# RWKV-7 in a hybrid backbone: the two directions of a chunk, instead of two chunks, on the two partition halves

## The chip, the cores and the metric

One core of a Trainium2 chip runs the whole network in one launch. The metric is the device time of one execution in microseconds (us). The engines are named as in the profile: PE (TensorE), ACT (ScalarE), DVE (VectorE), POOL (GpSimd) and SP (SyncE, which issues nearly all DMAs here).

## The reference, cut to what matters

Two layers of a hybrid block work on 512 latent and 256 context tokens of width 2048. One input projection feeds four branches (S5, windowed attention, RWKV-7, Hyena), each 512 wide, and an output projection merges them. The change touches RWKV alone. It has 8 heads of 64 channels and runs over time in both directions; per step and head, with state `S` (64 x 64):

```python
sa = jnp.einsum('bhij,bhj->bhi', state, -kk_t)
state = (state * w_t[:, :, None, :] + sa[..., None] * b_t[:, :, None, :]
         + v_t[..., None] * k_t[:, :, None, :])
y = jnp.einsum('bhij,bhj->bhi', state, r_t)
```

The context is run first, from a zero state, then the latents from the state that it leaves. The backward direction does the same over reversed time, and the two outputs are added.

## The kernel before

All matrices are f32. Where the trace counts matmul records, an f32 product of RWKV has two records and the split products of the projections (high and low parts, line 1645) have one each.

**RWKV in blocks.** The recurrence is computed in chunks of 64 steps. A block is two heads (128 channels, one of 4 channel tiles `c`) times 256 tokens (one of 3 groups `g`: context, first and second half of the latents), for both directions: 12 blocks per layer, 24 in all. Each block has three stages, `features`, `invert` and `chain`, and `run` traces them block after block. Most tiles have two buffers, so the stages of the next block may run ahead.

**`features`** (lines 288 to 368) loads r, k, kk, v (`ld`) and the half logits (`la`), makes decays with scans along time (line 312), scaled keys `kb` (lines 331, 332), then the scores `S`: per block 16 products of 64 contracted rows, 128 weight columns and 128 moving columns (line 340). For each direction `d` and head `h` four products lie on one half of the array's rows (`tile_position=(h * 64, 0)`), into one of two PSUM banks `mA`; DVE masks each bank into `S` (line 342). Then twelve 128 x 128 transposes (lines 351 to 353) go to `KU` by DVE and ACT (355 to 358), and 16 small products (line 365) give `BV`, through ACT (line 367). In these last the two parities `b` of chunk alternate between two quarters of the array, with rows and columns of 64 each, and all write one bank.

**`invert`** (lines 377 to 424) inverts the triangular scores: 31 steps of two operations on POOL (lines 398, 399) between DMAs that regroup the data, and 32 small products.

**`chain`** (lines 426 to 483) goes over the four chunks of a block in order, with the state `cur`. Before the change a pair of chunks (parities `b` 0 and 1) shares the 128 partitions, the even one's rows on one half, the odd one's on the other, and both directions of a chunk lie on the same half. Per chunk: two products of the state, one per direction, both into the same 64 output columns (line 439, here called fp); a DVE addition into `BV` (line 441); four products with the inverse, all on one quarter of the array (line 446, here called up); an ACT copy with the sign turned into `KU` (line 448); four products that make the state's increment (line 459, sp), whose two heads alternate between column halves; two DVE additions into the new state (line 466, with the decay at line 454); and the outputs y (lines 472, 475). fp, up and sp use one bank, `mU`, in turn.

**Order.** A planner that simulates the program fixes the order of each engine's instructions before the run. The class `Pace` adds order by hand: while RWKV runs, the input projections of the next branches (line 1645, three matmuls to a unit) fill PE, and a unit may not stand ahead of a given number of RWKV steps: fp, up and sp of each chunk count as steps (`lead`), the first step of a block allows 33 units in layer 0 and 27 in layer 1, every other 3 and 1. The weights of the filling units are split into high and low parts by ACT (line 1484) and by DVE or POOL (line 1485).

Of the kernel before, what the change touches and what calls it, by code (L numbers as in the profile page):

```python
# [37 lines left out]
# columns of the packed RWKV parameters  # L38
# [15 lines left out]
def pack_rw(I):  # L54
# [5 lines left out]
    wa = np.stack([I["rw_w2"], I["rw_a2"]], axis=2)  # layer, direction, (w, a), row, output  # L60
# [3 lines left out]
class K:  # L64
# [51 lines left out]
    def ring(self, shape=(128, 512)):  # L116
        """The banks beside those of the input projection, in turn."""
# [3 lines left out]
    def rms(self, y, sq, tmp, eng, eps, gate=None):  # L121
        """1 / sqrt(mean square + eps) over 4 channel tiles y, in sq (all of one width). With gate, which runs beside it: half of that, from 4 eps."""
# [19 lines left out]
class Pace:  # L142
    """Issue order on the tensor engine: units of a filling stream issue behind steps of a leading one."""
# [4 lines left out]
    def step(self, ins, allow):  # L148
        """ins leads; the units that come before it grow by allow."""
# [20 lines left out]
class RwFeed:  # L170
    """Token shift of the RWKV projections; r, k, kk, v and the half logits kept in both orders of time."""

    def __init__(self, k, l, raw):
# [5 lines left out]
        # 1 - mu_prev - mu_next, w0 / 2, a0 / 2, k_a / 2, 1 - k_a, 2 - k_a  # L179
# [11 lines left out]
        # r, k, kk, v and tanh of the half logits (decay, a), forward and reversed  # L191
# [7 lines left out]
    def store(self, d, z, ctx):  # L199
        """z [128, 769] (latent | - | context) into d [128, 2, NT], as it is and reversed."""  # L200
# [8 lines left out]
    def feed(self, j, lat, ctx):  # L209
        """Projection tile j (r 0-3, k 4-7, v 8-11, lora 12) in lat / ctx [128, n]: token shift."""  # L210
# [30 lines left out]
    def logits(self, lz):  # L241
        """tanh of half the decay and a logits of all channels: (high, low, high, low) x (high, high, low, low) in one product. In 8 parts."""
# [30 lines left out]
class Rwkv:  # L273
    """Bidirectional RWKV-7 over chunks of 64 steps; both directions advance together, each in its own order of time."""
# [13 lines left out]
    def features(self, c, g):  # L288
        """Scores and transposed operands of 4 chunks of two heads."""
# [10 lines left out]
        BV = t([128, 2, 4, 64], "rwBV", self.nbuf)  # L300
# [25 lines left out]
        # slots of a pair: K even | B even | B odd | K odd, in the place of k and kk  # L326
        kb = ld[:, 1:3].rearrange("p q d t -> p (q d t)").rearrange("p (x s t) -> p x s t", x=4, s=4)
        r4 = "p d (a b s) -> p (d a) b s"
        pi4 = pi.rearrange(r4, a=2, b=2)
        a4, kd4 = a.rearrange(r4, a=2, b=2), kd.rearrange(r4, a=2, b=2)  # L330
        V.tensor_tensor(kb[:, :, 1:3, :], a4, pi4, ALU.mult)
        V.tensor_tensor(kb[:, :, 0::3, :], kd4, pi4, ALU.mult)
# [10 lines left out]
        pc = PC.rearrange("p d (a b) -> p (d a) b", b=2).unsqueeze(3).to_broadcast([128, 4, 2, 64])  # L343
        # end-scaled K (natural), B (chunks of a pair exchanged)
        V.tensor_tensor(kd4, kb[:, :, 0::3, :], pc, ALU.mult)
        V.tensor_tensor(a4[:, :, ::-1, :], kb[:, :, 1:3, :], pc, ALU.mult)
        for d in range(2):
            for p in range(2):
                x = slice(p * 128, p * 128 + 128)
                pt = k.bank("mA", 2)  # L350
                nc.tensor.transpose(pt[:, 0:128], kd[:, d, x], C["ident"])
                nc.tensor.transpose(pt[:, 128:256], v[:, d, x], C["ident"])
                nc.tensor.transpose(pt[:, 256:384], a[:, d, x], C["ident"])
                ku = KU[:, d, p]
                V.tensor_copy(ku[0:64, 0], pt[0:64, 0:256].rearrange("p (a b) -> p a b", a=2))
# [1591 lines left out]
```

## Time and profile before

| | us |
|---|---|
| median of three runs | 3715.84 (3708.41 to 3725.21) |
| the profiled execution, its span | 3742.2 |
| PE busy in it | 3482.5 |
| RWKV of layer 0, about 740 to 1500 | 760 |
| RWKV of layer 1, about 2640 to 3320 | 680 |

The profile is of one execution, and nothing but the span stands for its time: the span from the first to the last instruction. A record of a matmul has its own length, but matmuls overlap, so what a group costs PE is its busy time divided by its count, or the length of a burst on the timeline (from the first start to the last end), not the mean of one. The granted clock is 1.00 where TensorE has 2.4 GHz and 0.50 where it has 1.2.

### The profile page before, as it was taken

The numbers are of one execution on the slowest core, as the hardware profiler recorded it, in microseconds if no ns is written. First come the engines' busy times: TensorE is split into PE (matmuls) and PEld (weight loads), VectorE is DVE, ScalarE is ACT, GpSimd is POOL, SyncE is SP. The second block draws the span as 40 slices with busy tenths as digits, with TensorE's granted clock in tenths as the row PEclk, the third lists the DMA queues.
The fourth block names the chain that finished last, engine by engine and source line by source line (L and its number), as shares of the span: only waits on it lengthen the run. The fifth ranks groups of instructions, "written<-read, shape, count | busy, mean of one in ns | idle before, by whom it ended". The sixth has DMA issues, their size and how long they took to land. (4 is left out here: it accounts for less than half of the span.)

```text
span 3742.2 us, 63165 instructions
## 1 busy us (share of the span) xinstructions
PE 3482.5 (93%) x23222; PEld 2692.6 (72%) x23222; DVE 2234.8 (60%) x4239; ACT 1491.1 (40%) x2875; POOL 1386.2 (37%) x2508
## 2 busy tenths in 40 slices
PE   5897899999999999999999978999999999999999
PEld 1465777777778777788777866776776767677867
DVE  7673666546555544366667664775466565546765
ACT  3344433434344433244313454443434443435522
POOL 5642664152435242000143424663434455411031
PEclk9998999999999999999999988999988998999999
DMA  7855344554445444543633325435533433435244
GB/s 241 273 174 157 106 115 126 174 159 112 138 133 144 134 135 132 160 129 113 216 113 101 111 86 151 130 102 170 171 89 109 123 99 112 120 119 185 66 158 121
DMA packets 546737, 515.12 MB, mean 138 GB/s; under 512 B 166425, under 2 KB 392506, under 8 KB 545532
## 3 DMA queue, kind: packets, MB, share of 16 engines
q1 hardware_dynamic: 546428, 511.08, 45.2%
q8 instruction: 184, 3.01, 0.3%
q14 instruction: 125, 1.02, 0.1%
HBM read 406.59 MB, written 100.93 MB: 136 GB/s over the span
## 5 line engine op out<-in xcount | busy, mean ns | idle before, releaser
L1645 PE MATMUL pin<-hxh,wh 128*128 128x512 f32 (+1 forms) x2624 | 988.9, 377 | 10.6 <-ACT ev L267 5.0
L1645 PE MATMUL pin<-hxh,wl 128*128 128x512 f32 (+1 forms) x2624 | 946.2, 363 | 13.7 <-POOL wl L1485 10.0
L1645 PE MATMUL pin<-hxl,wh 128*128 128x512 f32 (+1 forms) x2624 | 945.8, 361 | 0.0
L1484 ACT ACTIVATE wh<-wr 128x512 fp32r<-128x512 f32 x548 | 344.4, 629 | 828.3 <-PE pin L1645 389.5
L1645 PEld LDWEIGHTS pin<-hxh,wh 128*128 128x128 f32 x2624 | 506.7, 193 | 126.7 <-issue 32.3
L1645 PEld LDWEIGHTS pin<-hxh,wl 128*128 128x128 f32 x2624 | 505.5, 193 | 96.1 <-POOL wl L1485 12.9
L1645 PEld LDWEIGHTS pin<-hxl,wh 128*128 128x128 f32 x2624 | 508.1, 194 | 73.3 <-issue 5.3
L1485 DVE TENSOR_TENSOR wl<-wr,wh 128x512 fp32r<-128x512 f32 x434 | 318.6, 734 | 306.7 <-ACT wh L1484 290.1
L1485 POOL TENSOR_TENSOR wl<-wr,wh 128x512 fp32r<-128x512 f32 x114 | 159.0, 1395 | 868.9 <-ACT wh L1484 755.5
L398 POOL TENSOR_TENSOR rwtm<-rwAb,rwX 128x60 f32<-128x60 f32 (+24 forms) x744 | 258.2, 347 | 343.9 <-DMA rwAb<-rwAd 148.1
L1735 PE MATMUL pin<-yh,wl 128*128 128x512 f32 (+1 forms) x768 | 281.5, 368 | 6.5 <-DVE wl L1485 6.4
L1735 PE MATMUL pin<-yh,wh 128*128 128x512 f32 (+1 forms) x768 | 281.8, 368 | 3.5 <-ACT yh L1711 1.3
L399 POOL TENSOR_TENSOR rwX<-rwX,rwtm 128x60 f32<-128x60 f32 (+24 forms) x744 | 263.1, 354 | 57.4
L1735 PE MATMUL pin<-yl,wh 128*128 128x512 f32 (+1 forms) x768 | 280.5, 365 | 2.3 <-DVE yl L1712 2.0
L1735 PEld LDWEIGHTS pin<-yh,wl 128*128 128x128 f32 x768 | 145.9, 190 | 32.3 <-DVE wl L1485 9.7
L1735 PEld LDWEIGHTS pin<-yh,wh 128*128 128x128 f32 x768 | 145.9, 190 | 30.1 <-ACT yh L1711 3.8
L1735 PEld LDWEIGHTS pin<-yl,wh 128*128 128x128 f32 x768 | 146.2, 190 | 26.7 <-DVE yl L1712 3.4
L1739 DVE SCALAR_TENSOR_TENSOR xt<-pin,GT,xt 128x512 f32<-128x512 f32 (+1 forms) x144 | 93.8, 656 | 87.0 <-PE pin L1735 86.7
L1542 PE MATMUL pin<-wr,cs 128*32 128x128 f32 x2048 | 119.8, 290 | 15.5 <-DMA wr<-in_wada 11.7
L448 ACT ACTIVATE rwKU<-mU 64x256 f32<-64x256 f32 x96 | 36.2, 377 | 194.4 <-PE mU L446 193.4
L466 DVE TENSOR_TENSOR rwst<-rwst,mU 64x128 f32<-64x128 f32 x160 | 45.3, 283 | 87.4 <-PE mU L459 84.6
L340 PE MATMUL mA<-rwZR,rwld 64*128 64x128 f32 x768 | 91.7, 288 | 5.5 <-DVE rwS L342 4.5
(608 smaller groups left out, 6548.7 us busy)
## 6 DMA issues: line engine op xcount, KB each, us to landing
wr<-in_win SPq DMA_DIRECT2D x408, 256.0 KB
wr<-in_wada SPq DMA_DIRECT2D x256, 256.0 KB
ada<-in_wada SPq DMA_DIRECT2D x64, 512.0 KB
wr<-in_wo SPq DMA_DIRECT2D x128, 256.0 KB
rwld<-rwF SPq DMA_DIRECT2D x20, 1024.0 KB
rwF<-ev SPq DMA_DIRECT2D x64, 256.0 KB
xt<-in_xin SPq DMA_DIRECT2D x32, 384.0 KB
rwLA<-ev SPq DMA_DIRECT2D x32, 384.0 KB
```

The costliest lines, as they stand in the source:

```text
L340: nc.tensor.matmul(pss[:, p, b, :], kb[hr, d * 2 + p, 2 * b:2 * b + 2, :].rearrange("p b s -> p (b s)"), ZR[hr, d, :, tt * 64:tt * 64 + 64 ...
L398: E.tensor_tensor(tm, Ab[:, 0:s, s:s + 1].to_broadcast([128, s, w]), X[:, s:s + 1, m:8].to_broadcast([128, s, w]), ALU.mult)
L399: E.tensor_tensor(X[:, 0:s, m:8], X[:, 0:s, m:8], tm, ALU.subtract)
L448: nc.scalar.activation(KU[rB, :, p, b, 1, :], up[rB].rearrange("p d a b -> p d (a b)"), AF.Copy, scale=-1.0)
L466: V.tensor_tensor(new[hs, :, hs], new[hs, :, hs], sp[hs], ALU.add)
L1484: nc.scalar.activation(h, raw, AF.Copy)
L1485: (nc.gpsimd if i % 4 == 3 else nc.vector).tensor_tensor(l, raw, h.bitcast(F32), ALU.subtract)
L1542: nc.tensor.matmul(ps[32 * j:32 * j + 32, :], self.cs[:, q * 4 + j, :], w3[:, j], start=q == 0, stop=q == 3, tile_position=(0, 32 * j))
L1645: mm.append(nc.tensor.matmul(ps, w[:, c], x[:, t], start=a, stop=b))
L1735: nc.tensor.matmul(ps, w[:, c], y[:, t], start=a, stop=b)
L1739: nc.vector.scalar_tensor_tensor(x[:, t], ps, self.GT[l][:, s, j:j + 1], x[:, t], ALU.mult, ALU.add)
```

## The change

The tiles of a block are laid out by chunk first, and the two directions take the place of the two chunks of a pair on the partition halves. In `features` the scores of a chunk pair are gathered in two banks at once, head 0 in one, head 1 in the other, and consecutive products alternate between the two halves of the array's rows. `v` is copied into chunk order (a new ACT copy of 128 x 512 per block, into the place of `pi`) before it is transposed. In `chain`, the two fp products go to different column halves, the four up products alternate between two quarters of the array, the addition into `BV` is one of 128 x 128 instead of 64 x 256, and the copy into `KU` is two of 64 x 128, direction 0 on ACT and direction 1 on DVE. The counts of products, transposes and steps, `invert`, `Pace` and its numbers stay. The rest of the diff takes comments away.

```diff
-        S = t([128, 2, 4, 2, 128], "rwS", self.nbuf)  # direction, (pair, head), parity
-        KU = t([128, 2, 2, 2, 2, 128], "rwKU", self.nbuf)  # direction, pair, parity, (K/B | V/U)
+        S = t([128, 4, 2, 2, 128], "rwS", self.nbuf)
+        KU = t([128, 4, 2, 2, 128], "rwKU", self.nbuf)
...
-        for d in range(2):
+        for cp in range(2):
+            pss = [k.bank("mA", 2, (128, 2, 2, 128)) for _ in range(2)]
+            for cc in range(2):
+                ck = cp * 2 + cc
+                for d in range(2):
+                    for h in range(2):
+                        hr = slice(h * 64, h * 64 + 64)
+                        nc.tensor.matmul(pss[h][:, cc, d, :], kb[hr, ck, 2 * d:2 * d + 2, :].rearrange("p b s -> p (b s)"),
+                                         ZR[hr, d, :, ck * 64:ck * 64 + 64], start=True, stop=True, tile_position=(h * 64, 0))
             for h in range(2):
-                hr = slice(h * 64, h * 64 + 64)
-                pss = k.bank("mA", 2, (128, 2, 2, 128))
-                for p in range(2):
-                    for b in range(2):
-                        tt = p * 2 + b
-                        nc.tensor.matmul(pss[:, p, b, :], kb[hr, d * 2 + p, 2 * b:2 * b + 2, :].rearrange("p b s -> p (b s)"),
-                                         ZR[hr, d, :, tt * 64:tt * 64 + 64], start=True, stop=True, tile_position=(h * 64, 0))
-                V.tensor_tensor(S[:, d, h::2], pss, C["rwmask"].unsqueeze(1).unsqueeze(1).to_broadcast([128, 2, 2, 128]), ALU.mult)
+                V.tensor_tensor(S[:, cp * 2:cp * 2 + 2, h], pss[h], C["rwmask"].unsqueeze(1).unsqueeze(1).to_broadcast([128, 2, 2, 128]), ALU.mult)
...
+        ke, be, ve = [x.rearrange("p d t -> p (d t)").rearrange("p (c d t) -> p c d t", c=4, d=2) for x in (kd, a, pi)]
+        nc.scalar.activation(ve, chunks(v), AF.Copy)
...
             if cur is not None:
-                fp = k.bank("mU", 1, (128, 2, 2, 64))
+                fp = k.bank("mU", 1, (128, 2, 64))
                 for d in range(2):
-                    m = nc.tensor.matmul(fp[rB, d].rearrange("p a b -> p (a b)"), ZR[:, d, 0, t0:t0 + 64], cur[:, d], start=True, stop=True, tile_position=(0, rB.start))
+                    rB = self.rows(d)[0]
+                    m = nc.tensor.matmul(fp[rB].rearrange("p a b -> p (a b)"), ZR[:, d, 0, t0:t0 + 64], cur[:, d], start=True, stop=True, tile_position=(0, rB.start))
                 self.lead(m, ck == 0)
-                V.tensor_tensor(BV[rB, :, us], fp[rB], BV[rB, :, us], ALU.add)
-            fs = BV[:, :, us]
-            up = k.bank("mU", 1, (128, 2, 2, 64))
+                V.tensor_tensor(BV[:, ck], fp, BV[:, ck], ALU.add)
+            up = k.bank("mU", 1, (128, 2, 64))
+            for h in range(2):
+                for d in range(2):
+                    rB = self.rows(d)[0]
+                    m = nc.tensor.matmul(up[rB, h, :], XT[rB, ck * 2 + h, :], BV[rB, ck, h, :], start=True, stop=True, tile_position=(rB.start, rB.start))
+            self.lead(m, ck == 0 and cur is None)
             for d in range(2):
-                for h in range(2):
-                    m = nc.tensor.matmul(up[rB, d, h, :], XT[rB, d * 4 + p * 2 + h, :], fs[rB, d, h, :], start=True, stop=True, tile_position=(rB.start, rB.start))
-            self.lead(m, ck == 0 and cur is None)
-            nc.scalar.activation(KU[rB, :, p, b, 1, :], up[rB].rearrange("p d a b -> p d (a b)"), AF.Copy, scale=-1.0)
+                rB = self.rows(d)[0]
+                o, u = KU[rB, ck, d, 1, :], up[rB].rearrange("p a b -> p (a b)")
+                if d:
+                    V.tensor_scalar(o, u, -1.0, None, ALU.mult)
+                else:
+                    nc.scalar.activation(o, u, AF.Copy, scale=-1.0)
```

## Rows read from the trace of the kernel before

**Rows 1.** Busy time of each engine over the whole span, from the page.
```profile
PE 3482.5 (93%) x23222; PEld 2692.6 (72%) x23222; DVE 2234.8 (60%) x4239; ACT 1491.1 (40%) x2875; POOL 1386.2 (37%) x2508
```

**Rows 2.** Stretches: length, busy us of each engine (x instructions), granted clock, DMA share, GB/s.
```profile
740.00:1500.00 760.00, 740.09 (x6389) 592.65 (x6382) 410.51 (x823) 297.54 (x591) 290.59 (x774) 0.98 0.47 136
...
2640.00:3320.00 680.00, 637.72 (x4611) 475.33 (x4610) 377.51 (x749) 277.12 (x542) 303.30 (x777) 0.90 0.40 114
```

**Rows 3.** The PE instructions that gather RWKV's scores, fp and up: records, busy us, mean ns.
```profile
L340 PE MATMUL mA<-rwZR,rwld 64*128 64x128 f32 x768 | 91.7, 288 | 5.5 <-DVE rwS L342 4.5 <-DVE rwld L332 1.0
...
L446 PE MATMUL mU<-rwBV,rwXT 64*64 64x64 f32 x768 | 68.1, 232 | 7.7 <-DVE rwBV L441 7.5 <-ACT rwXT L424 0.2
L439 PE MATMUL mU<-rwst,rwZR 128*64 128x128 f32 x352 | 60.9, 299 | 13.9 <-DVE rwst L466 12.3 <-DVE rwst L464 1.4
```

**Rows 4.** Waits of PE in 740:1500: waiting line, releaser, us, times, longest.
```profile
PE mU L439 <- DVE rwst L466: 3.5, 2, 2.9
...
PE mA L340 <- DVE rwS L342: 2.1, 1, 2.1
```

**Rows 5.** Waits of PE in 2640:3320.
```profile
PE mU L439 <- DVE rwst L466: 8.9, 6, 2.4
PE mU L446 <- DVE rwBV L441: 7.1, 8, 1.4
...
PE mU L459 <- ACT rwKU L448: 1.4, 1, 1.4
```

**Rows 6.** Chain of waits, shares of 2640:3320 by line.
```profile
by line: PE pin L1645 28.2%; POOL rwX L399 8.6%; POOL rwtm L398 8.0%; issue 6.3%; DMA rwla<-rwLA 5.4%; PE mA L340 3.3%; DMA rwXd<-rwX 2.8%; PE mU L446 2.6%; POOL wl L1485 2.1%; PE mY L472 2.0%; PE mU L439 1.8%; DVE rwL L312 1.6%; DMA rwAb<-
```

**Rows 7.** Timeline of PE, one up burst and one run of 16 score records: start, length.
```profile
1110.84 0.68 PE L446 MATMUL mU<-rwBV,rwXT 64*64 64x64 f32 x8
1111.44 1.71 PE L340 MATMUL mA<-rwZR,rwld 64*128 64x128 f32 x16
```

**Rows 8.** Timeline of PE, a score burst of 8 alone.
```profile
1115.11 1.16 PE L340 MATMUL mA<-rwZR,rwld 64*128 64x128 f32 x8
```

**Rows 9.** Timeline of PE, bursts on alternating quarter tiles, and fp between.
```profile
2757.26 0.80 PE L365 MATMUL mA<-rwKU,rwS 64*64 64x64 f32 x20
2757.99 0.65 PE L439 MATMUL mU<-rwst,rwZR 128*64 128x128 f32 x4
...
2758.93 0.56 PE L365 MATMUL mA<-rwKU,rwS 64*64 64x64 f32 x12
```

**Rows 10.** Timeline of PE, attention values: alternating column halves in the shape of fp.
```profile
1799.12 0.44 PE L1425 MATMUL mA<-atPT,atvt 128*64 128x128 f32 x4
```

**Rows 11.** ACT groups by line: busy us, mean ns, idle before.
```profile
L1484 ACT ACTIVATE wh<-wr 128x512 fp32r<-128x512 f32 x548 | 344.4, 629 | 828.3 <-PE pin L1645 389.5 <-PE pin L1735 220.4 <-DMA wr<-in_win 132.6
...
L448 ACT ACTIVATE rwKU<-mU 64x256 f32<-64x256 f32 x96 | 36.2, 377 | 194.4 <-PE mU L446 193.4
```

**Rows 12.** DVE groups by line.
```profile
L342 DVE TENSOR_TENSOR rwS<-mA,c_rwmask 128x512 f32<-128x512 f32 x96 | 63.5, 683 | 39.6 <-PE mA L340 39.2
...
L466 DVE TENSOR_TENSOR rwst<-rwst,mU 64x128 f32<-64x128 f32 x160 | 45.3, 283 | 87.4 <-PE mU L459 84.6
...
L441 DVE TENSOR_TENSOR rwBV<-mU,rwBV 64x256 f32<-64x256 f32 x88 | 36.9, 419 | 57.6 <-PE mU L439 56.5
```

**Rows 13.** Instructions of line 340: waits placed on PE's weight queue, ns.
```profile
L340 PEldq EVENT_SEMAPHORE  x22: 51/51/51, 740.1 to 3224.6; - x22
```

**Rows 14.** Timeline of PE, a wait in layer 1.
```profile
2766.19 0.93 PE L439 MATMUL mU<-rwst,rwZR 128*64 128x128 f32 x4 [1.35 <-DVE rwst L466]
```

**Rows 15.** The 5 us from 2770 on, columns as in rows 2.
```profile
2770.00:2775.00 5.00, 5.00 (x26) 3.19 (x24) 1.16 (x4) 1.01 (x2) 2.63 (x5) 0.50 0.09 28
```

**Rows 16.** Timeline of DVE ahead of that wait.
```profile
2762.33 1.80 DVE L312 TENSOR_TENSOR_SCAN rwL<-rwd,rwla 128x64 f32<-128x64 f32 x8
...
2765.45 0.59 DVE L466 TENSOR_TENSOR rwst<-rwst,mU 64x128 f32<-64x128 f32 x2
```

**Rows 17.** Timeline of ACT in the same block.
```profile
2761.95 0.38 ACT L448 ACTIVATE rwKU<-mU 64x256 f32<-64x256 f32 x1 [0.15 <-PE mU L446]
```

More of the change, by code (lines that the diff above doesn't have):

```diff
@@ L343, in features @@
[L343 to L355, printed above, removed]
-                nc.scalar.activation(ku[64:128, 1], pt[64:128, 0:256].rearrange("p (a b) -> p a b", a=2), AF.Copy)
-                nc.scalar.activation(ku[0:64, 1, 0, :], pt[0:64, 256:384], AF.Copy)
-                nc.scalar.activation(ku[64:128, 0, 0, :], pt[64:128, 256:384], AF.Copy)
@@ L359, in features, with chunks @@
-        pb = k.bank("mA", 2, (128, 2, 4, 64))
-        for d in range(2):
-            for u in range(4):
-                p, hs = u // 2, slice(u % 2 * 64, u % 2 * 64 + 64)
-                for b in range(2):
-                    rB, rK = self.rows(b)
-                    nc.tensor.matmul(pb[rB, d, u, :], S[rK, d, u, b, 0:64], KU[rK, d, p, b, 1, hs], start=True, stop=True,
+        def chunks(x):
+            return x.rearrange("p d (c t) -> p c d t", c=4)
+        V.tensor_tensor(kb[:, :, 1:3, :], chunks(a), chunks(pi), ALU.mult)
@@ new lines, in features @@
+        pc = PC.rearrange("p d c -> p c d").unsqueeze(3).to_broadcast([128, 4, 2, 64])
+        ke, be, ve = [x.rearrange("p d t -> p (d t)").rearrange("p (c d t) -> p c d t", c=4, d=2) for x in (kd, a, pi)]
+        nc.scalar.activation(ve, chunks(v), AF.Copy)
+        V.tensor_tensor(ke, kb[:, :, 0::3, :], pc, ALU.mult)
+        V.tensor_tensor(be[:, :, ::-1, :], kb[:, :, 1:3, :], pc, ALU.mult)
+        for ck in range(4):
+            pt = k.bank("mA", 2)
+            nc.tensor.transpose(pt[:, 0:128], ke[:, ck].rearrange("p d t -> p (d t)"), C["ident"])
+            nc.tensor.transpose(pt[:, 128:256], ve[:, ck].rearrange("p d t -> p (d t)"), C["ident"])
+            nc.tensor.transpose(pt[:, 256:384], be[:, ck].rearrange("p d t -> p (d t)"), C["ident"])
+            ku = KU[:, ck]
+            V.tensor_copy(ku[0:64, 0], pt[0:64, 0:256].rearrange("p (a b) -> p a b", a=2))
+            nc.scalar.activation(ku[64:128, 1], pt[64:128, 0:256].rearrange("p (a b) -> p a b", a=2), AF.Copy)
+            nc.scalar.activation(ku[0:64, 1, 0, :], pt[0:64, 256:384], AF.Copy)
+            nc.scalar.activation(ku[64:128, 0, 0, :], pt[64:128, 256:384], AF.Copy)
@@ L366, in features @@
+        pb = k.bank("mA", 2, (128, 4, 2, 64))
+        for ck in range(4):
+            for h in range(2):
+                hs = slice(h * 64, h * 64 + 64)
+                for d in range(2):
+                    rB, rK = self.rows(d)
+                    nc.tensor.matmul(pb[rB, ck, h, :], S[rK, ck, h, d, 0:64], KU[rK, ck, d, 1, hs], start=True, stop=True,
                                      tile_position=(rK.start, rB.start))
@@ L387, in invert @@
         P1 = XR
-        S8 = S.rearrange("p d u b x -> p (d u) b x")
+        S8 = S.rearrange("p c h d x -> p (c h) d x")
         grp = [(b, q, self.rows(b)[0].start + 32 * q) for b in (1, 0) for q in range(2)]
@@ L458, in chain @@
                         hs = slice(h * 64, h * 64 + 64)
-                        m = nc.tensor.matmul(sp[hs, d, :], KU[:, d, p, b, 0, hs], KU[:, d, p, b, 1, hs], start=True, stop=True, tile_position=(0, h * 64))
+                        m = nc.tensor.matmul(sp[hs, d, :], KU[:, ck, d, 0, hs], KU[:, ck, d, 1, hs], start=True, stop=True, tile_position=(0, h * 64))
                 self.lead(m)
@@ L474, in chain @@
                         hs = slice(h * 64, h * 64 + 64)
-                        nc.tensor.matmul(y[hs], KU[:, d, p, b, 1, hs], S[:, d, p * 2 + h, b, 64:128], start=cur is None, stop=True, tile_position=(0, h * 64))
+                        nc.tensor.matmul(y[hs], KU[:, ck, d, 1, hs], S[:, ck, h, d, 64:128], start=cur is None, stop=True, tile_position=(0, h * 64))
         if full:
```

13 lines of the change are left out of this document (4 added, 9 removed).

## The prediction, made before the changed kernel was run

> **What bounds the kernel now.** I read the page's first part before anything else: PE is busy for 93% of the span, the next engine for 60% [rows 1]. So what shortens PE's work can shorten the time, but only where PE is what ends last. The change acts while RWKV runs, so next came the stretches: in layer 0, PE is busy for 740.1 of 760 us at a granted clock of 0.98; in layer 1 for 637.7 of 680 at 0.90 [rows 2]. The reader should see two things. Layer 0 has 2.6% of slack on PE, layer 1 has 6.2%. And 0.90 means that PE spent 20% of layer 1's stretch at 1.2 GHz, which is 136 us for the work of 68; in layer 0 it is 4%, 30 us for the work of 15.
>
> Third, the groups of PE's lines. The products that the change rearranges are the scores (91.7 us), up (68.1) and fp (60.9), 221 us in all [rows 3]. The others of RWKV keep their shape and order. Fourth, the waits of PE: in layer 0 a few us in all for RWKV's handoffs [rows 4], in layer 1 more, and there the handoffs through DVE are the dear ones, 8.9 and 7.1 us, while the one through ACT costs 1.4 [rows 5]. Last, the chain of waits in layer 1: 17% of it is POOL's inversion, and scores, up and fp have 3.3, 2.6 and 1.8% [rows 6], 52 us of 680. Half of their PE time there (110 of 221) is thus on the chain by 47%.
>
> **The change, part by part.** *Up.* 96 bursts of 8 records, all on one quarter of the array. One takes 0.68 us [rows 7]. The nearest row with alternating quarters is line 365, in the same shape: 20 records in 0.80 us and 12 in 0.56, so 0.03 a record, and 8 would take 0.44 [rows 9]. That is 0.24 us less, times 96: 23 us. *Fp.* 88 bursts of 4 records in one column half, 0.65 us each [rows 9]. Line 1425 has the same shape on alternating halves, 4 in 0.44 [rows 10]: 0.21 times 88 is 18 us. *Scores.* 768 records are 48 groups of 16, at 91.7 us in all [rows 3] or 1.91 us each. No row has row halves that alternate record by record. But a run of 16 in the old order, 8 on one half and then 8 on the other, takes 1.71 us [rows 7], where 8 alone take 1.16 [rows 8]: the second half began before the first was done. With the two in turn I take the 1.16 of one half for both, 0.75 less, times 48: 36 us. The bounds are nothing and these 36; a loss is excluded by the same run of 16, which is shorter than two of 8 though part of it ran side by side. The sum is 77 us of PE, 38 in each layer.
>
> How much of it arrives: where PE is busy, its share. Layer 0 gives 38 x 0.97 = 37 us. Layer 1 gives 38 x 0.94 = 36 at best and, by the chain, 18 at worst. I take 36 and put the waits in as costs of their own.
>
> *The copy into KU.* It now waits for up on two engines, and sp for both. On ACT it took 377 ns for 64 x 256 [rows 11]; half of it, and the DVE half by the 283 ns of a 64 x 128 operation [rows 12], take less, so the copy itself gains 0.1 us. But sp now waits for DVE, as fp and up do already. What is queued behind the DVE copy while it waits for up: the state's decay (line 454), the next block's scans and masks, and the splits of line 1485 that feed the filling matmuls. What may stand before it is the same work. I price the third handoff as the other two: 8 us in layer 1 instead of 1.4, 6.6 more; in layer 0 the fp handoff's 3.5 [rows 4]. A stall also costs clock. In layer 1, 68 us are lost to the low clock beside 42 us of idle time, 1.6 per us; in layer 0, 15 beside 20, 0.75. So 6.6 x 2.6 = 17, and 3.5 x 1.75 = 6. Bounds: from a gain of 0.1 us per chunk, 10 us in all, to the slower case below.
>
> *A second wait on PE.* sp has a single releaser now. With two, one wait goes onto the weight queue, as 22 did for the scores at 51 ns each [rows 13]: 88 x 51 ns = 4.5 us; nothing if it stands in idle time.
>
> *The scores' handoff.* The first two groups now fill both banks, and the third needs the second bank back. The wait for the mask stands at 2.1 us in layer 0 [rows 4]; the planner can put filling matmuls there. I add 3 us for both layers, bounds 0 and 24 x 0.68 = 16, one mask of line 342 for each block [rows 12].
>
> *The copy of v.* 24 ACT copies of 128 x 512, 629 ns each by line 1484 [rows 11]: 15 us. They start when `kb` is done and are needed by the transposes, behind four masks on DVE, 2.7 us [rows 12], and two multiplications. I cost them at nothing; 15 us if that cover is gone.
>
> *The addition into BV.* 88 times 419 ns for 64 x 256; at 128 x 128 I take the 283 ns of a 128-element operation [rows 12]. 12 us of DVE and 0.13 us per chunk of latency go. With 96 copies at 283 ns, DVE has 15 us more work and is idle for 40% of the span [rows 1]: nothing. `Pace` counts units and steps, and both stay.
>
> The sum: 37 + 36 - 17 - 6 - 4.5 - 3 = 42.5, say 42 us. The profiled execution has 3742.2 us and is 26 longer than the median of 3715.84, with nothing known around the span; it would come to 3700, and I take the same 42 off the median: 3674 us.
>
> **The rivals.** *Layer 1 is bound by its chain (R1).* If POOL's inversion, the DMAs and the handoffs set layer 1's length, the 36 us there become idle time while the costs stay: 37 - 30.5 = 6 us, 3710. For it: 17% of the chain is POOL, and the low clock. Against: PE is busy for 94% of that stretch, and the handoffs through fp, up and `BV` themselves get shorter.
>
> *The overlap is not there for up and fp (R2).* Two quarters might not be able to write one bank together, and two column halves might not load weights together. PE then saves the scores alone: 18 x 0.97 + 18 x 0.94 - 30.5 = 4 us, 3712. Against it stand line 365, whose two quarters write one bank at 0.03 us a record [rows 9], and line 1425 [rows 10]. The first is what the Trainium skill states in "TensorEngine Tiling (Array Packing)", Restrictions and Gotchas: different row tiles cannot access the same PSUM bank simultaneously. The second is the Trainium skill's "TensorE: Matmul & The Clock Gate", Part 3, by which weight loads overlap with matmuls in flight only where the row group differs. The rows of this trace differ from both, with 0.03 us a record on one bank and 0.44 us for a burst of fp's shape, so both rules together get a small chance. By the first alone the saving on PE would be 23 us less, by the second alone 18.
>
> *Everything arrives (R3).* The third handoff costs nothing, the shorter copies take waits away, and the low clock is no more frequent: 37 + 36 and the 7.1 us that up waits for line 441 in layer 1 [rows 5], 80 us, 3636.
>
> *Slower: DVE's queue stops the chain (R4).* At 2766.19 PE's fp had waited 1.35 us for line 466 [rows 14], and the granted clock stood at 0.50 from then on [rows 15], because DVE did 1.80 us of the next block's scans at 2762.33 and more before it came to line 466 at 2765.45 [rows 16]. In the same block ACT made the copy into `KU` at once, at 2761.95 [rows 17]. Had its half been on DVE behind the scans, it would have ended at 2764.13 + 0.28, 2764.41, instead of 2762.33: 2.1 us later. If that hits one chunk in four, 12 a layer, it costs 12 x 2.1 x 2.6 = 66 us in layer 1 and 12 x 2.1 x 1.75 = 44 in layer 0. With 7.5 for the other costs that is 117 against 73: 44 slower, 3760. It decides from about 14 such hits in the 96 chunks (65.5 over a mean of 4.6); with 18 the kernel is slower by over 0.5%. Against it: the planner sees the copy as part of the older block, which it traced first, and line 441 stands on DVE already with 7.1 us of waits in layer 1.
>
> **How the numbers follow.** Forecast 0.57, at 3640 to 3700 with 3674 likeliest; R1 0.15, R2 0.04, R3 0.10, R4 0.14. Faster or slower means by over 0.5%, 18.6 us, about what a measurement of this kernel can tell from no change: below 3697 or above 3734. Faster: nearly all of the forecast (0.55), R3, and a little of R1 (0.02): 0.67. Slower: R4 less its mild cases, 0.13. Same: 0.20. For the range I leave out half of R3 at the bottom and most of R4 at the top: 3632 to 3724. It takes in the bounds of the costs above, 15 us for the copy of v and 16 for the masks, from the forecast up to 3705.
>
> **What would show it.** Right: in the groups of PE's lines the scores fall from 91.7 to about 55 us, up from 68 to 46, fp from 61 to 42; bursts of up at 0.44 us and of fp at 0.44 on the timeline; runs of 16 score records at about 1.2. PE's busy time in the RWKV stretches falls by some 70 us and its idle time grows by less than half of that. The waits of sp name DVE, some 8 us in layer 1. Wrong: bursts as long as before (R2); shorter bursts with idle time of the same size, and POOL and DMA with more of layer 1's chain (R1); waits of sp for DVE of 20 us or more a layer and a granted clock below 0.95 in layer 0 (R4). What I can't see from here is the order that the planner makes of it; a new order may move the time by itself, both ways.

## The result, and the profile after

The changed kernel takes 3783.09 us (median of 4 runs, 3772.59 to 3793.6); the kernel before took 3720.53 beside it. The ratio is 1.0167 [1.0135, 1.0199]: slower by 1.7%, where 3674 was forecast, and above the top of the range, 3724.

The page after, as in [rows 1], and the stretches, as in [rows 2] (each a little longer, since RWKV is):

```profile
PE 3453.6 (91%) x23222; PEld 2658.4 (70%) x23222; DVE 2235.3 (59%) x4335; ACT 1497.8 (40%) x2899; POOL 1394.1 (37%) x2508
```
```profile
740.00:1530.00 790.00, 742.60 (x6423) 588.47 (x6422) 411.83 (x869) 301.72 (x606) 296.26 (x775) 0.94 0.46 131
2665.00:3365.00 700.00, 617.83 (x4622) 453.87 (x4620) 380.19 (x798) 279.05 (x554) 308.35 (x778) 0.89 0.39 111
```

PE's busy time fell by 29 us, but in layer 0 PE is now idle for 47 of 790 us, where it was idle for 20 of 760, and the granted clock fell from 0.98 to 0.94. In layer 1 the idle time went from 42 of 680 to 82 of 700.

The groups of PE's lines that [rows 3] shows of before, records, busy us and mean ns; the products did become shorter:

```profile
L340 PE MATMUL mA<-rwZR,rwld 64*128 64x128 f32 x768 | 85.4, 315 | 9.5 <-DVE rwld L332 5.7 <-DVE rwS L343 3.7
L445 PE MATMUL mU<-rwBV,rwXT 64*64 64x64 f32 x768 | 49.0, 243 | 5.6 <-DVE rwBV L440 4.4 <-ACT rwXT L425 0.9
L464 PE MATMUL mU<-rwKU 128*64 128x64 f32 x704 | 43.2, 245 | 13.7 <-DVE rwKU L451 13.6
L438 PE MATMUL mU<-rwst,rwZR 128*64 128x128 f32 x352 | 40.7, 310 | 10.6 <-DVE rwst L471 10.6
```

One burst of up, one of fp and one run of 16 score records on the timeline, as in [rows 7, 9]: 0.45 us for 0.68, 0.44 for 0.65, 1.16 for 1.71.

```profile
1121.30 0.45 PE L445 MATMUL mU<-rwBV,rwXT 64*64 64x64 f32 x8
1128.76 0.44 PE L438 MATMUL mU<-rwst,rwZR 128*64 128x128 f32 x4
...
2703.73 1.16 PE L340 MATMUL mA<-rwZR,rwld 64*128 64x128 f32 x16
```

So something else lengthened RWKV. POOL's inversion is what needs the scores next, so the view to read is the waits of POOL: waiting tile and line, releaser, us, times, longest. The kernel before, 740:1500:

```profile
POOL rwtm L398 <- DMA rwAb<-rwAd: 73.6, 5, 22.9
POOL rwtm L398 <- issue: 69.5, 4, 21.9
POOL rwtm L398 <- DMA qkv<-ev: 27.1, 1, 27.1
```

The changed kernel, 740:1530:

```profile
POOL rwtm L399 <- DMA rwAb<-rwAd: 234.9, 8, 36.8
...
POOL rwtm L399 <- DMA rwfin<-rwLA: 31.6, 1, 31.6
POOL rwtm L399 <- issue: 30.2, 1, 30.2
```

The waits that end with the broadcast of the scores (`rwAb`) are three times as long. The profile puts some of the same waits down to other releasers; with all of them the inversion's first line waits 308 us where it waited 185, and in layer 1 116 where it waited 104. POOL's wait is longer, then, but this view does not say what delays the broadcast.

And the chain of waits of 2665:3365, whose row of before is [rows 6]: POOL's two lines go from 16.6% to 21.8%, the DMAs around the inversion (rwAd, rwAb, rwXd, rwXP) have 12.4% where they had 6.0, and filling matmuls (line 1650, 1645 before) fall from 28.2% to 21.9%.

```profile
by line: PE pin L1650 21.9%; POOL rwX L400 11.2%; POOL rwtm L399 10.6%; issue 6.9%; DMA rwXd<-rwX 4.7%; DMA rwXP<-rwXd 3.5%; SPq L402 3.3%; DMA rwla<-rwLA 2.7%; PE mY L477 2.5%; ACT rwXT L406 2.3%; DMA rwAd<-rwS 2.2%; DMA rwAb<-rwAd 2.0%; P
```

*Where the time lies.* I cut each trace at the first operation of features (line 307) and the last up of each layer, and split each piece into PE's busy time weighted by the granted clock ("work"), the rest of its busy time ("low clock") and idle time. Outside RWKV the two kernels differ by 10 us (2251 and 2241). The two RWKV stretches together, us:

| kernel | stretches | work | low clock | idle |
|---|---|---|---|---|
| before | 1491 | 1349 | 78 | 64 |
| after | 1542 | 1294 | 115 | 132 |

The change took 55 us of work away and put 37 of low clock and 68 of idle time in its place. These are the two profiled executions, which differ by 41 us; the medians differ by 63, because the profiled execution of before lies 24 us above the median of all runs of that kernel, 3718.

*The loop.* S, KU and ZR have two buffers, so block i's scores wait until the chain of block i-2 is done. A loop of waits thus spans two blocks: end of a chain, first score, last mask, broadcast issued, POOL's first and last step, products, first up, last up. Its parts as means over blocks 2 to 11 of a layer, from starts and ends of those lines in the traces, us, layer 0 / layer 1:

| part | before | after |
|---|---|---|
| end of chain to first score | 15.9 / 12.9 | 15.6 / 12.4 |
| first score to last mask | 9.1 / 11.5 | 11.8 / 13.5 |
| last mask to rwAb issued | 3.7 / 3.8 | 6.1 / 6.0 |
| rwAb issued to POOL's first step | 4.4 / 4.6 | 4.2 / 4.1 |
| POOL's inversion | 27.2 / 29.7 | 27.8 / 30.2 |
| to the first product on its result | 11.4 / 13.6 | 10.5 / 11.2 |
| to the first up | 9.8 / 10.6 | 11.0 / 10.7 |
| first up to last up | 39.8 / 21.5 | 40.1 / 21.6 |
| sum | 121.3 / 108.2 | 127.1 / 109.7 |

In layer 1 the sum grows by little: 10 of the 19 us by which that stretch is longer have come by the end of its second block, which these means leave out. Two things matter. The chain itself, the last part, did not become shorter although its bursts did. And from the first score to the broadcast it takes 5.1 and 4.2 us more. What is new there is the order of SP's DMA issues around the broadcast. Before, the load of the next block's `ld` (L303, 1 MB) follows the broadcast:

```profile
1053.74 1.80 SPq L391 DMA_DIRECT2D rwAd<-rwS  x4
1056.88 0.54 SPq L392 DMA_DIRECT2D rwAb<-rwAd  x1
1061.82 0.35 SPq L1629 DMA_DIRECT2D wr<-in_win  x1
1062.97 0.53 SPq L303 DMA_DIRECT2D rwld<-rwF  x1
```

After, it stands right ahead of the four small stores of the scores, and the broadcast, which needs these, leaves 3.9 us behind the last of them instead of 1.3:

```profile
1012.96 0.54 SPq L303 DMA_DIRECT2D rwld<-rwF  x1
1013.89 1.92 SPq L392 DMA_DIRECT2D rwAd<-rwS  x4
1016.30 0.35 SPq L1634 DMA_DIRECT2D wr<-in_win  x1
1017.75 0.40 SPq L1545 DMA_DIRECT2D wr<-in_wada  x1
1019.72 0.55 SPq L393 DMA_DIRECT2D rwAb<-rwAd  x1
```

It can stand there because of line 347. Before, v was transposed straight from `ld`, which was in use until the last transpose, and the next load left some 9 us behind the end of the last mask. Now v is copied, and `ld` is free once the last scores have been read from it.

### The profile page after: what moved, and what is told of

It reads as the page before. It is cut to its first block, busy times and chain, and to the rows that moved or that the text cites. A ratio compares the mean times of both kernels' runs of the same rounds, so it can differ in the third digit from the quotient of the medians.

```text
span 3782.8 us, 63229 instructions
## 1 busy us (share of the span) xinstructions
PE 3453.6 (91%) x23222; PEld 2658.4 (70%) x23222; DVE 2235.3 (59%) x4335; ACT 1497.8 (40%) x2899; POOL 1394.1 (37%) x2508
## 5 line engine op out<-in xcount | busy, mean ns | idle before, releaser
L400 POOL TENSOR_TENSOR rwX<-rwX,rwtm 128x60 f32<-128x60 f32 (+24 forms) x744 | 273.8, 368 | 56.8 <-POOL rwtm L399 0.2
L406 ACT ACTIVATE rwXT<-rwXP 32x256 f32<-32x256 f32 x96 | 63.3, 660 | 126.1 <-DMA rwXP<-rwXd 124.6
L1547 PEld LDWEIGHTS pin<-wr,cs 128*32 128x32 f32 x2048 | 48.8, 111 | 64.7 <-DMA wr<-in_wada 27.2
```

Of the source, the lines that this page charges most:

```text
L400: E.tensor_tensor(X[:, 0:s, m:8], X[:, 0:s, m:8], tm, ALU.subtract)
L406: nc.scalar.activation(XT[r:r + 32, :, 32 * q:32 * q + 32].rearrange("p u (m g) -> p u m g", g=4), XR[r:r + 32].rearrange("p u (g m) -> p ...
L1547: nc.tensor.matmul(ps[32 * j:32 * j + 32, :], self.cs[:, q * 4 + j, :], w3[:, j], start=q == 0, stop=q == 3, tile_position=(0, 32 * j))
```

## The experiments

The theory that came out of these rows: the copy of v frees `ld` early, and the next load's transfer delays the small stores, the inversion and with it the loop. Its rivals: gathering the scores in two banks, the third handoff through DVE (R4 of the prediction), the copy's own time, and a new order by the planner. The letters in the expectations differ from run to run. In the first four, A holds both the early load and the gathering in two banks, B is the handoff through DVE, and C the planner's order. Later A or A1 is the early load alone, and A2 or B what the text beside it says.

*e1_no_v_copy.* No copy; two products with the identity, one to each column half, bring v of both directions from `ld` into place:

```diff
-        nc.scalar.activation(ve, chunks(v), AF.Copy)
...
-            nc.tensor.transpose(pt[:, 128:256], ve[:, ck].rearrange("p d t -> p (d t)"), C["ident"])
+            for d in range(2):
+                nc.tensor.matmul(pt[d * 64:d * 64 + 64, 128:256], v[:, d, ck * 64:ck * 64 + 64], C["ident"], start=True, stop=True, tile_position=(0, d * 64))
```

> The changed kernel without the copy of v: v is transposed straight from the loaded tile, by two products of 64 columns per chunk on the two column halves. The loaded tile is then held until the transposes, as before the change. Theory A (RWKV's blocks run in a loop of waits that spans two blocks; the change put two delays into it: the gathering of scores in two banks at once, and the load of the next block, 1 MB, which the copy of v sets free before the scores' own small DMAs): the time from the last mask to the first step of the inversion falls from about 10.2 us to about 8.2, and the time by about 20 us, from 3783 to about 3760. Theory B (the copy into KU on DVE stops DVE's queue, and that alone costs the time): nothing moves by over 8 us. Theory C (the planner's new order costs it, whatever the edit): a move of either sign, with no change in the time from mask to inversion.

3716.0 us, 0.9985 [0.9963, 1.0007]: the whole loss is gone, 67 us where A had said 20, and no gain is left. Its PE work is dearer than the changed kernel's: v's products and the two transposes beside them (lines 351 to 354) keep PE busy for 86 us, where the three transposes of the changed kernel take 49.

*e2_old_gather* gathers the scores one bank at a time, one head after the other, as before; *e3_both* is e1 with that.

```diff
-            pss = [k.bank("mA", 2, (128, 2, 2, 128)) for _ in range(2)]
-            for cc in range(2):
...
-                    for h in range(2):
-                        hr = slice(h * 64, h * 64 + 64)
+            for h in range(2):
+                hr = slice(h * 64, h * 64 + 64)
+                pss = k.bank("mA", 2, (128, 2, 2, 128))
+                for cc in range(2):
...
```

> The changed kernel with the scores gathered one bank at a time again (four products of one head, then the mask, and so on), in the new layout. Theory A: the time from the first score to the last mask of a block falls from 11.8 us (layer 0) and 13.5 (layer 1) to about 9 and 11.5, PE's busy time on scores goes up from 85 to about 92 us, and the time falls by 20 to 30 us all the same, to about 3757. Theory B: the time stays at 3783, or goes up by the scores' PE time. Theory C: a move of either sign that the two stretches of a block do not explain.

> Both edits: no copy of v, and scores gathered one bank at a time. What is left of the change is the chain (fp, up, the addition into BV, the copy into KU on two engines). Theory A: the loop is back to the length of before, less what fp, up and the addition save in the chain: between 3700 and 3725. Theory B: at least 3765, for the copy into KU on DVE is still there. Theory C: anywhere, with the parts of the loop not those of before.

e2: 3775.56, 1.016 [1.0135, 1.0185]; e3: 3726.95, 1.0027 [1.0012, 1.0043]. With either gathering the copy's removal is worth 49 to 67 us, and the gathering itself 8 to 11, once in each direction, where A had said 20 to 30. So of A's two delays the early load is the one that counts. B is out too: by it e3, in which DVE still makes its half of the copy into `KU`, would have stayed above 3765.

*e4_before_v_copy*: the kernel before, with a copy of v into `pi` that its transposes then read.

> The kernel before with one thing added: v is copied by ACT into the place of pi, and transposed from there, so that the loaded tile is free earlier. No other operation changes. Theory A: the next block's load is issued ahead of the scores' small DMAs instead of 9 us behind the last mask, the time from the last mask to the inversion grows from 8.2 to about 10 us, and the kernel is slower by 10 to 25 us. Theory B and theory C with the change's own parts: 24 ACT copies of about 0.6 us beside an ACT that is idle 60% of the time, no change beyond 8 us.

3794.17, 1.0218 [1.0185, 1.025]: the copy alone, in the old layout, makes it 76 us slower, three times what A had said at most. What costs the time is not the new layout.

*e9_copy_ld_held*: the changed kernel with its copy, but the last chunk's v is transposed straight from `ld` (the two products of e1, for `ck == 3` alone), so that `ld` is held as before.

> The changed kernel with the copy of v kept, whole, but with the last chunk's v transposed straight from the loaded tile, so that this tile is held until then, as before the change. It has the copy without the early load. Theory A1 (the early load costs: SP issues the next block's 1 MB between the masks and the scores' small DMAs): the load moves back to about 9 us behind the last mask, mask to inversion is 8 us again, and the time is 3716 to 3730, as without the copy. Theory A2 (the copy itself costs: it stands on ACT and waits for DVE's multiplications, and the splits of the filling weights wait behind it): the time stays at 3765 or more, with first score to last mask still near 12 us.

3721.53, 1.0014 [0.9993, 1.0035]. The copy is there in full (24 on ACT) and costs next to nothing, as predicted; its release of `ld` costs 62 us. SP's order of it has the load back behind the broadcast:

```profile
1000.95 1.80 SPq L396 DMA_DIRECT2D rwAd<-rwS  x4
1004.02 0.55 SPq L397 DMA_DIRECT2D rwAb<-rwAd  x1
...
1010.72 0.53 SPq L303 DMA_DIRECT2D rwld<-rwF  x1
```

*e10_before_v_own_tile*: the kernel before, v in a tile and a DMA of its own (256 KB), so that the other 768 KB are free early without any copy.

> The kernel before with v loaded into a tile of its own (two DMAs, 768 and 256 KB, instead of one of 1 MB), so that r, k and kk are free before the transposes. It has the early load without a copy. Theory A1: the load of 768 KB is issued ahead of the scores' small DMAs, the time from mask to the inversion's broadcast grows from 3.7 us to 5 or 6, and the kernel is slower by 30 to 75 us. Theory A2: no change beyond 8 us. Half each: slower by 20 to 40.

3748.13, 1.0087 [1.0054, 1.012]: 30 us slower from the earlier load of three quarters of the bytes. In e4 the load leaves at the same moment and costs 46 us more; whether the last quarter of the bytes makes that or the copy, no run separates.

*e11_load_by_pool*: the changed kernel with `nc.gpsimd.dma_start` for the load, to take it out of SP's order.

> The changed kernel with the load of r, k, kk and v issued by POOL instead of SP. The load stays early and its bytes still share the DMA engines, but it no longer stands in SP's order ahead of the scores' DMAs. If SP's order and its slots are what the early load costs, mask to broadcast falls from 6.1 to about 3.7 us and the time by 20 us or more; if it is the sharing of bandwidth, or theory A2, it stays near 3780 (POOL's own issue may add some).

3812.35, 1.0256 [1.0205, 1.0307], still slower. Two views bear on it. POOL now stands idle ahead of the load, 275.5 us in all, about half of it until PE has read the scores' operands out of `ld`. What this costs the kernel is not measured by itself:

```profile
L303 POOL DMA_DIRECT2D rwld<-rwF x24 | 22.0, 918 | 275.5 <-PE mA L340 135.4
```

And the broadcast is as late as in the changed kernel, though SP issues nothing between the stores and it. POOL's timeline, then SP's:

```profile
1139.77 0.93 POOL L303 DMA_DIRECT2D rwld<-rwF  x1 [26.98 <-PE pin L1547]
```
```profile
1140.67 2.52 SPq L392 DMA_DIRECT2D rwAd<-rwS  x4
1147.98 0.53 SPq L393 DMA_DIRECT2D rwAb<-rwAd  x1
```

The broadcast leaves 4.8 us behind the last store. Of the 20 blocks (2 to 11 of each layer), 13 had the load out up to 2.3 us ahead of the first store, and the gap is 2.9 to 5.6 us in all of them; in three of the 13 SP issues nothing in between, and these have 4.8 to 5.3. In all 13 the broadcast leaves 0.6 to 2.5 us behind the landing of the load. In five blocks the load had gone 4.8 to 12.4 us ahead, and four of these have 1.2 to 1.6 us, the fifth 4.0; the two last blocks of the layers, with no load, have 1.3. So it is not SP's order but the transfer in flight that delays the stores. The Trainium skill states in "DMA: Bandwidth & Descriptors", Issuing engines are not separate DMA queues, that transfers run on the same 16 DMA engines and interleave, whichever engine started them. This run agrees with that: the gap is 2.9 to 5.6 us with POOL issuing the load, and 3.1 to 5.3 in the blocks of the changed kernel whose load SP issued as closely ahead.

*e12_no_copy_act_ku*: e1, with both halves of the copy into `KU` on ACT.

```diff
-                if d:
-                    V.tensor_scalar(o, u, -1.0, None, ALU.mult)
-                else:
-                    nc.scalar.activation(o, u, AF.Copy, scale=-1.0)
+                nc.scalar.activation(o, u, AF.Copy, scale=-1.0)
```

> The changed kernel without the copy of v (as in the first of these runs), and with both halves of the copy into KU on ACT. Without the copy of v the waits of sp for DVE are 10.2 us, and DVE sits waiting for ACT ahead of its half. If the third handoff through DVE costs what the prediction said (17 us in layer 1, 6 in layer 0), the time falls by 10 to 25 us, to 3690 to 3705, below the kernel before; if not, it stays within 8 us of 3716: two ACT copies of 0.27 us follow each other, 0.17 us more than one of 0.38.

3735.91, 1.0053 [1.0033, 1.0074], 20 us slower than e1, which neither of the two expectations allowed. The wait for `KU` moved rather than went. Waits of PE in 2590:3330 for the chain's handoffs, e1 and then e12 (lines 438, 445 and 464 of e1 are 438, 445 and 461 here):

```profile
PE mU L464 <- DVE rwKU L451: 10.2, 11, 1.8
PE mU L445 <- DVE rwBV L440: 7.5, 8, 1.7
...
PE mU L438 <- DVE rwst L471: 2.3, 3, 1.1
```
```profile
PE mU L438 <- DVE rwst L468: 11.4, 6, 3.5
PE mU L445 <- DVE rwBV L440: 10.9, 7, 2.7
...
PE mU L461 <- ACT rwKU L450: 3.9, 4, 1.8
```

*e16_late_part* was to be the version that keeps everything of the changed kernel and loses nothing: `ld` is held by the copy itself, whose last part waits for a place.

```diff
-        nc.scalar.activation(ve, chunks(v), AF.Copy)
+        vs = chunks(v)
+        nc.scalar.activation(ve[:, 0:3], vs[:, 0:3], AF.Copy)
...
-            nc.tensor.transpose(pt[:, 128:256], ve[:, ck].rearrange("p d t -> p (d t)"), C["ident"])
+            nc.tensor.transpose(pt[:, 128:256], ve[:, ck % 3].rearrange("p d t -> p (d t)"), C["ident"])
+            if ck == 0:
+                nc.scalar.activation(ve[:, 0], vs[:, 3], AF.Copy)
```

> The changed kernel, but the copy of v is made in two parts: chunks 0 to 2 at once, chunk 3 into the place of chunk 0 when chunk 0's transpose has read it. The loaded tile is held until then, PE has exactly the products of the changed kernel, and no transposes of v by column halves as in the earlier versions without the copy. Theory A (the early release costs the time; PE's saved work is there, but in part turns into waits): the load is again issued some 9 us after the last mask, the broadcast of line 393 some 3.5 us after it, RWKV's idle time falls from 132 to about 90 us and what the low clock costs there from 115 to about 80; work at full clock stays at 1294. Span about 3783 - 42 - 35 = 3706, median 3700 to 3718. Rival B (the copy on ACT and the order of the scores cost the time, the release is only beside it): no faster than 3760.

3758.4, 1.0131 [1.0098, 1.0164], a miss for A as I had put it. Chunk 0's transpose comes early, and the load left 2.9 us behind the last mask, between the stores and the broadcast, not 9. There it holds up the broadcast itself, from whose issue to POOL's first step it takes 5.0 and 5.8 us in the two layers, 4.0 and 4.1 in e9.

*e19_last_part*: the same with `min(ck, 2)` for `ck % 3`, and chunk 3's part copied into place 2 when `ck == 2`.

> The run before held the loaded tile only until chunk 0's transpose, and the next load went out 2.9 us after the last mask, between the stores of line 392 and the broadcast of line 393, instead of 10 us after it. Here chunk 3's v goes into the place of chunk 2 once chunk 2's transpose has read it; PE's products are again those of the changed kernel. Theory A (the time follows the moment of the load): the load goes out 7 to 10 us after the last mask, behind the broadcast; from the last mask to POOL's start it takes 7.5 us as with the load held until the last transpose, instead of 9.6; median 3705 to 3725. Rival B (what the held tile gained earlier came from the transposes of v by column halves, not from the load's moment): no faster than 3745.

3733.0, 1.0052 [1.0035, 1.007]: the load leaves 8.5 us behind the mask, as expected; the time is 8 us above the top of what A expected, 50 below the changed kernel with the same products on PE, and 25 below e16. With 0.5% over the kernel before it is slower than that, clear of noise. Rival B, no faster than 3745, is out.

*e15_before_half_inv* and *e17_late_part_half_inv*: `range(31, 0, -2)` for `range(31, 0, -1)` in the inversion, in the kernel before and in e16. They leave out every second step of the inversion, so they measure the loop and do not compute the result.

> The kernel before with every second of the 31 steps of POOL's inversion left out (the result is then another one; PE, DVE, ACT and the DMAs keep all their work). If the loop of waits (mask, broadcast, inversion, products, chain) sets RWKV's length, POOL's 27 to 30 us of it fall by about 13, and RWKV's idle time and clock loss, 64 + 78 us, fall by more than half: 3640 to 3670. If PE's work alone sets it, the idle time has other releasers and the time stays within 15 us of 3718.

> The late part of the copy and half the inversion together. If the changed layout's saving on PE (work at full clock in RWKV 1349 to 1294 us) is lost only because the loop of waits takes its place, then with a shorter loop it arrives: 30 to 55 us below the kernel before with half the inversion. If it is lost for another reason (DVE's handoffs, the clock by itself), the two come out within 15 us of each other.

e15: 3692.59, 0.9953 [0.9934, 0.9971]; e17: 3718.27, 1.0015 [0.9992, 1.0038]. Both misses. RWKV's stretches became 100 and 89 us shorter, but 44 and 56 of that came back outside as filling matmuls that no longer found room there. And with the shorter inversion e17 is still 26 us slower than e15. This is not shown to be the layout's doing alone, since e17 has e16's load, 3 to 4 us behind the mask. But of the 2.8 and 3.6 us by which its loop is longer (layer 0 and 1), the chain has 1.7 and 2.3, and the waits of PE in 2590:3330, e15 and then e17, point to its handoffs through DVE.

```profile
PE mU L439 <- DVE rwst L466: 4.5, 4, 2.0
...
PE mU L446 <- DVE rwBV L441: 2.0, 3, 1.6
PE mI L415 <- DVE rwXP L411: 1.7, 1, 1.7
```
```profile
PE mU L448 <- DVE rwBV L443: 12.8, 5, 6.0
PE mU L467 <- DVE rwKU L454: 12.5, 8, 3.4
PE mI L419 <- DVE rwXP L415: 12.1, 3, 5.1
```

*All of them by the moment of the load.* Load: its issue after the end of the last mask (median), minus is ahead of it. Gap: end of the last store's issue to the broadcast's issue (mean). Each over blocks 2 to 11 of layer 0 / layer 1. RWKV: both stretches of the profiled execution, as work + low clock + idle. Median: of all executions, us; the profiled one lies 24 us above it for before and 6 to 11 below it for e3, e9, e10 and e16. e15 and e17, with half the inversion, are not in the table.

| run | load | gap | RWKV | median |
|---|---|---|---|---|
| e1 | 10.7 / 9.6 | 1.3 / 1.8 | 1481 = 1361 + 58 + 61 | 3716 |
| before | 9.5 / 8.9 | 1.5 / 1.7 | 1491 = 1349 + 78 + 64 | 3718 |
| e9 | 10.2 / 9.1 | 1.3 / 1.7 | 1487 = 1313 + 81 + 93 | 3722 |
| e3 | 10.8 / 10.7 | 1.5 / 1.8 | 1486 = 1361 + 63 + 62 | 3727 |
| e19 | 8.5 / 8.5 | 1.7 / 1.5 | 1498 = 1311 + 85 + 102 | 3733 |
| e12 | 10.1 / 9.0 | 1.5 / 1.6 | 1492 = 1330 + 78 + 85 | 3736 |
| e10 | -0.7 / -0.8 | 2.9 / 3.1 | 1504 = 1344 + 83 + 77 | 3748 |
| e16 | 2.9 / 2.8 | 2.5 / 1.8 | 1526 = 1305 + 94 + 128 | 3758 |
| e2 | -0.7 / -0.7 | 3.6 / 3.5 | 1544 = 1320 + 108 + 115 | 3776 |
| after | -1.7 / -0.9 | 3.1 / 3.6 | 1542 = 1294 + 115 + 132 | 3783 |
| e4 | -0.7 / -0.7 | 4.0 / 3.5 | 1553 = 1353 + 101 + 99 | 3794 |
| e11 | -0.6 / -1.0 | 4.0 / 3.3 | 1581 = 1304 + 123 + 153 | 3812 |

Two things are read from it. The six kernels with the load 8.5 us or more behind the mask are the six fastest, and all with an earlier one are slower, in either layout. Every edit also gives the planner a new order; that the order alone should have sorted the kernels like this is unlikely, but no run holds it fixed. And in RWKV the time doesn't follow PE's work: from before to e19 38 us of work go and 38 of idle time come.

## Why the prediction was wrong

*The step that failed* is "The copy of v", costed at nothing, 15 us if its cover is gone. As time of ACT that was right: e9 has the copy and the time of before within its interval. What I didn't ask is what the copy sets free. It ends the use of `ld`, `ld` is what the next load waits for, and that load's 1 MB hold up the four 32-KB stores of the scores. The runs give the price: 50 us (after to e19, with the same products on PE; 43 by their ratios to the kernel before), 62 (after to e9), 67 (after to e1), 76 (before to e4); an early transfer of three quarters of the bytes without any copy makes 30 (e10). The rows had shown enough to ask: the chain of waits has POOL's inversion and its DMAs [rows 6]. I followed every instruction that the change adds, but not the DMA that one of them releases.

From after to e9 the loop's sum falls by 3.1 and 5.8 us per two blocks. Last mask to POOL's first step falls from 10.3 to 7.3 and from 10.1 to 7.6, first score to last mask from 11.8 to 10.2 and from 13.5 to 12.5; other parts give some of it back in layer 0. The first of these is shown, by the gap and by e11's blocks. Why the masks come later too is not settled: no run changed that alone.

*PE's terms.* Fp: 60.9 to 40.7, forecast 42. Up: 68.1 to 49.0, forecast 46, with bursts of 0.45. Scores: 91.7 to 85.4, forecast 55; this term was mis-sized, and in part by its working: it set a mean over all groups, 1.91 us, against a single burst of 1.16, where the old order's own run of 16, 1.71, would have given 0.55 less a group and 26 us. A run of 16 that takes the heads in turn lasts the 1.16 us of [rows 8], as forecast. But of the 48 groups only 26 are such runs by themselves (23 at the full clock, 1.25 us in the mean). In others the second pair of a block comes in parts of 8, probably because its two banks come free one after the other: 14 runs of 8, the 7 at the full clock at 1.09 us each. And 14 runs of all lengths fell to the low clock. The first and the second pair of one block, all of it at 1.2 GHz, filling matmuls between:

```profile
1064.59 2.08 PE L340 MATMUL mA<-rwZR,rwld 64*128 64x128 f32 x16 [0.18 <-DVE rwld L332]
...
1069.38 2.07 PE L340 MATMUL mA<-rwZR,rwld 64*128 64x128 f32 x8
...
1072.68 2.07 PE L340 MATMUL mA<-rwZR,rwld 64*128 64x128 f32 x8
```

So 46 of the 77 us were there. R2 is refuted: up's records alternate between two quarters on one bank, fp's between column halves. By the Trainium skill's "TensorEngine Tiling (Array Packing)", Restrictions and Gotchas, up would have stayed as long as before, and by the Trainium skill's "TensorE: Matmul & The Clock Gate", Part 3, fp; the rows, 0.45 and 0.44 us, differ from both. In both bursts the records now start in pairs, 7 ns apart in the median, where they started 59 (up) and 130 (fp) apart.

*How much arrives* failed as well, and would have without the copy. I let PE's share of busy time, 97 and 94%, stand for the share of a saving that arrives. With the load back in its place, e19 and e9 save 38 and 36 us of work in RWKV, and idle time grows by 38 and 29. That is R1 in both layers, with its signs: shorter bursts, idle time of about the same size, and more of layer 1's chain of waits for POOL and the DMAs. Its 3710 lies 12 us below e9. A share of busy time tells nothing here because the planner's filling matmuls keep PE busy while the loop waits; they are what is moved when the loop changes, as e15 shows.

*The handoffs.* The third one through DVE costs sp 13.6 us of waits (2.8 and 10.8), where I had 10.1, 23 with the clock: the size was fair. But the copy itself, which was to gain 0.1 us, became longer. I let its halves on ACT and DVE run side by side, and in none of the 96 chunks do they: DVE's half starts at the earliest 32 ns after the end of ACT's, 33 in the median, and the profile gives ACT's half as what it waited for. The DVE group by line:

```profile
L451 DVE TENSOR_SCALAR rwKU<-mU 64x128 f32<-64x128 f32 x96 | 26.6, 278 | 89.7 <-ACT rwKU L453 89.3
```

The whole copy is done 0.80 us behind the last record of up in the median (1.39 in the mean), where it was done 0.42 behind (0.58). By the median that takes back 0.38, by the mean all, of the 0.57 us a chunk that fp, up and the addition into `BV` gave. It fits the chain's unchanged length, but no run has the halves side by side, so it is not shown to be its cause. R4 is refuted as the cause: e3 keeps DVE's half and loses 9 us in all, and e12 takes DVE out, and the waits turn up at the other two handoffs. Of R4's signs, the 20 us of waits a layer did not come; a granted clock below 0.95 in layer 0 did (0.94). But the low clock costs layer 0 12 and 16 us in e1 and e3, which keep DVE's half, 14 before and 44 after, so that half alone does not bring it. The second wait on PE came 8 times at 51 ns, not 88 times, and PE's waits for the masks went from 4.5 to 3.7 us, so as waits these two terms were near nothing. The addition into `BV` takes 288 ns for 419, as forecast. The low clock cost more than thought, 37 us more in RWKV, 30 of them in layer 0, where idle time grew too.

*The median and the profiled execution.* I took the difference of 26 us as unexplained. The profiled execution of before has a mean granted clock of 0.952, executions within 4 us of its median 0.955 to 0.961; 0.3 to 0.9% of PE's 3482 us is 10 to 31. So the clock can account for it, this profile of before flatters a change by about that much, and a comparison goes by medians.

No version that keeps the whole inversion was faster than the kernel before; e1 and e9 equal it.

## What to carry to other kernels

For each copy that a change adds, ask which buffer it frees and what transfer that releases, and look where on the issuing queue this will stand; a large prefetch just ahead of small stores on the critical path costs more than the copy. Holding a tile until the small transfers are out can be worth keeping. Where a copy is split over two engines, look at the start times: here the second half waited for the first. And where filling work keeps an engine busy, its busy share says nothing of what a saving is worth: find the loop of waits, and see whether the shortened work is a part of it or is covered by its handoffs.

## What the runs showed of the hardware

- Four stores of 32 KB, and a broadcast that needs them: in 14 of 20 blocks of the kernel before the broadcast leaves 1.2 to 1.4 us behind the end of the last store's issue, in the other six 1.7 to 3.3. Where a 1-MB load went out up to 2.3 us ahead of the first store, it leaves 3.1 to 5.3 us behind (the changed kernel, SP issuing the load, 13 blocks) and 2.9 to 5.6 (e11, POOL issuing it, 13 blocks).
- On two quarters of the array with one bank (up) and on two column halves (fp), records start in pairs 7 ns apart in the median; on one quarter or one half 59 and 130 ns.
- Score records whose row halves alternate one by one: 16 in 1.16 us, as long as 8 on one half alone at the same clock.
